# Raw weights in single blocks through four half-size buffers, a changed account of landings and readiness, and state-gate weights read again instead of kept

## The chip, the core and the metric

The kernel runs on one core of one Trainium2 chip. The metric is device time in microseconds (us) of one execution. The engines are named as the profile names them: PE (TensorE; PEld its weight loads), DVE (VectorE), ACT (ScalarE), POOL (GpSimd) and SP (SyncE, which here issues DMAs only).

## The reference

One layer of a hybrid encoder: 16 learned meta tokens stand ahead of 2048 frames of 1024 channels. The input is normalized and goes through one projection with seven parts of 512 columns; the result feeds a convolution group and a stick-breaking attention group, whose outputs are joined, projected, normalized and added to the input.

```python
u = rms_norm(h, pre_g)
proj = u @ w_in                      # 1024 x 3584
glu_a, glu_b, conv_gate, q, k, v, sb_gate = jnp.split(proj, ...)
c = glu_a * jax.nn.sigmoid(glu_b)
c = causal_depthwise_conv(c, conv_w, conv_b)          # width 31
c = jax.nn.silu(layer_norm(c, conv_ln_g, conv_ln_b))
c = (c @ w_pw2 + b_pw2) * jax.nn.silu(conv_gate)
s = stick_breaking_attention(heads(q), heads(k), heads(v))   # 8 heads of 64
s = s * jax.nn.silu(sb_gate)
mixed = jnp.concatenate([c, s], axis=-1) @ w_out      # 1024 x 1024
return h + rms_norm(mixed, post_g)

# within the attention
z = q @ k.T * scale
log_stay = where(visible, log_sigmoid(-z), 0)
tail = cumsum(log_stay, reverse=True) - log_stay
a = where(visible, exp(log_sigmoid(z) + tail), 0)
out = a @ v
```

All arrays are float32. The kernel gets near that accuracy by splitting each operand into a high part (rounded to the matmul's format) and a low part (the rest): high x high, high x low and low x high are three matmuls into one PSUM bank.

## The kernel before

**Tiling.** The frames are worked on in four chunks of 512 (`TC`), 128 rows at a time. For chunk c, `attention(c)` is the main stream of PE work: per head and block of keys it computes scores (`T<-kk,q`), turns the running products that DVE scans back (`T<-ident,pr`) and sums values (`av<-ah,vk`, `av<-al,vk`). Beside it a second stream, the fill, does the state gate `sb_gate(c)`, the output projection of chunk c - 1, the convolution's norm (`conv_norm`, with the transposes `T<-ident,acc`) and gate of chunk c, and the input projection of chunk c + 1 (`mm<-uh,w`, `mm<-ul,w`). The first input projection stands alone at the start (0 to about 140 us). By the trace the state gates are stored at 152 to 173, 372 to 400, 674 to 706 and 1018 to 1060 us, at the start of each chunk's fill.

**Who sets the order.** The program is written out by hand at build time. `Clock` and `Engine` hold an account with a cost for every instruction: when a tile is ready, when a buffer is free, how far each engine has come. `merge` and `either` take from the streams the one whose next piece is due (`need` gives that time), so PE's order is fixed by the account. Small work on other engines is a `Later`: what it reads, what it writes, a date before which it isn't issued, and the tag of a buffer that it needs. On the chip each engine runs its instructions in that fixed order and waits for what isn't there, and all that stand behind wait with it.

**Weights.** A weight block is 128 x 512 numbers. A raw block comes by `sp.dma_start` from `wpack` into a `wr` buffer. `split` makes the two parts: ACT copies the high part (`w<-wr`), POOL, or DVE for seven blocks at the start, subtracts it (`w<-wr,w`). They lie side by side in a `w` slot. Blocks that are needed in later chunks are written by POOL's queue to `wscr` in DRAM after the first split in chunk 0's fill or later, and the next uses load both parts at once (`w<-wscr`, 512 KB). There are four `w` slots (`WB`) and two `wr` buffers of two blocks (`RAWS`); when no raw block is left, the `wr` buffers serve as two more slots. In the trace the first such load is at 445 us. `weights` takes the next blocks for a product; `release` gives a slot back and calls `prepare` for the next block.

**Other names that the change touches.** `measure_later` loads 128 rows of x into a `q` buffer (`q<-x`) and has ACT sum their squares (`ev<-q`). `load_first_in` starts the kernel; there `times` multiplies the first x by the rate of each frame, the product standing in `pr` tiles. `turn` transposes the differences of the values (`T<-ident,ev`), which POOL has made from ACT's copy of the value projection (`ev<-mm`). `meta_v` brings the meta tokens' values into `vm`, sixteen loads in a row. `load_q` and `load_k` bring a head's queries and keys.

Of the kernel before, what the change touches and what calls it, by code (L numbers as in the profile page):

```python
# [11 lines left out]
F32 = mybir.dt.float32  # L12
F32R = mybir.dt.float32r
# [25 lines left out]

EV, WB, RAWS, PR, EHL = 5, 4, 2, 9, 4  # L40

# [126 lines left out]
class Engine:  # L168
# [7 lines left out]
    def __getattr__(self, name):  # L176
        call = getattr(self.engine, name)

        def issue(out, *args, **kw):
# [28 lines left out]
            return call(out, *args, **kw)  # L208
# [48 lines left out]
def trunk(ctx: ExitStack, tc: tile.TileContext, x, xturn, xlater, meta, cpack, post_g, wpack, out):  # L257
# [54 lines left out]
    def PT(tag, shape):  # L312
# [4 lines left out]
        return t  # L317

    def need(*aps, tag=None, given=None, evs=0, n=1):

        def at():
            if given and not given():
                return 1e6
            t = max([clock.at(a) for a in aps] + [0.0])
            if tag:
                t = max(t, clock.next_free(tag, n))
            if evs:

                t = max(t, clock.next_free("ev", evs) - 1.0)
            return t + 0.1

        return at
# [198 lines left out]
    at = {key: i for i, key in enumerate(slab_keys())}  # L533
    todo_raw = deque(zip(whole[::2], whole[1::2]))
    raws, ready, held, tags = deque(), deque(), [], deque()

    def load_raw(most=RAWS):

        while todo_raw and len(raws) < most:
            a, b = todo_raw.popleft()  # L540
            assert at[b] == at[a] + 1
            raw = T("wr", [P, 2, 4 * P], RAWS)
            sp.dma_start(raw, wpack[at[a] : at[a] + 2].rearrange("i p n -> p i n"))
            raws.append([raw, 0])

    def prepare(most=WB):

        while most and todo_w:
            if tags.count("w") < WB:
                tag, bufs = "w", WB  # L550
# [7 lines left out]
            both = T(tag, [P, 2, 4 * P], bufs, F32R)[:, :, :n]  # L558
            if kept:
                sp.dma_start(both.bitcast(F32), place[key][:, :, :n])  # L560
            else:
                if not raws:
                    load_raw()
                raw, i = raws[0]

                def keep_it(key=key, both=both):
                    when(
                        lambda: pool.dma_start(place[key], both.bitcast(F32)), [both[:, 1]]
                    )

                split(
                    raw[:, i], both[:, 0], both[:, 1],

                    dve if len(todo_w) in FIRST else pool,
                    keep_it if save else None,
                )
                raws[0][1] += 1
                if i:
                    raws.popleft()
                    when(  # L580
                        lambda: load_raw(min(RAWS, len(raws) + 1)), [],
                        date=0.0 if len(todo_w) in FIRST else pe.now + 2.0, tag="wr",
                    )
            ready.append(
                (key, [both[:, i].rearrange("p (k n) -> p k n", n=key[2]) for i in range(2)])
            )

# [54 lines left out]
    def load_first_in():  # L642
# [3 lines left out]
        uh, ul = u_now  # L646
        raw = T("wr", [P, 2, 4 * P], RAWS)
        raws.append([raw, 0])
        a, b = todo_raw.popleft()
        sp.dma_start(raw[:, 0], wpack[at[a]])  # L650
        sp.dma_start(cp, cpack)
# [4 lines left out]
        for k in range(KD):  # L656
            ts.append(T("pr", [P, TC], PR))
            sp.dma_start(ts[k], xturn[:, k, NM:])
            when(lambda k=k: part_in(0, k, ts[k], uh, ul), [ts[k], cp])
            if k == 0:  # L660
                sp.dma_start(raw[:, 1], wpack[at[b]])

# [49 lines left out]
        def spread():  # L712
# [101 lines left out]
    def measure_later(n):  # L814
# [18 lines left out]

        when(square, [t], [later[:, n : n + 1]], tag="ev")

# [53 lines left out]
    def qk_proj(c, g, scr, with_meta):  # L889
        for j in range(NJ):  # L890
# [99 lines left out]
    def values(c):  # L990
# [3 lines left out]
        for j in range(NJ):  # L994
# [27 lines left out]
            def turn(dv, j, rows, t0, nb):  # L1022
# [3 lines left out]
                for b in range(0, nb, 2):  # L1026
                    n = min(2, nb - b)
                    part = T("mixs", [P, 2, 4, HD], 8, F32R)[:rows, 0:n]
                    hi, lo = part[:, :, 0::3, :], part[:, :, 1:3, :]
                    d = pt[:, b : b + n].rearrange("p b (h d) -> p b h d", d=HD)  # L1030
                    act.activation(hi, d, AF.Copy)
# [25 lines left out]

    def meta_v():
        for j in range(NJ):
            force(f"v{j}")  # L1060
        for h in range(NH):
            e, j = h % 2, h // 2
            rows = slice(e * HD, (e + 1) * HD)
            for i in range(2):
                blk = (0 if i == 0 else 1) if e == 0 else (3 if i == 0 else 2)
                sp.dma_start(
                    vm[h * NM : (h + 1) * NM, i, j, rows].bitcast(F32),
                    vscr[j, 0:NM, blk * HD : (blk + 1) * HD],
                )

# [189 lines left out]
    def attention(c, mixs):  # L1260
# [156 lines left out]
        for i in range(len(order) + 1):  # L1417
            u = None
            if i < len(order):
                h, kc = order[i]  # L1420
                u = dict(h=h, kc=kc, diag=kc == c, kk=kk, a=[], at=[])
                if i + 1 < len(order):
                    if order[i + 1][0] != h:
                        heads[h + 1] = load_q(c, h + 1)
                    kk = load_k(*order[i + 1])
            for b in range(NTB if u else len(flips)):
                if u:
# [18 lines left out]
            if i == 1:  # L1446
# [10 lines left out]
                if c == 0:  # L1457
                    in_us(15.0, meta_v, outs=[vm])
            done = u
# [434 lines left out]
    with tc.manual_schedule(  # L1894
# [15 lines left out]
        for c in range(NCH):  # L1910
# [62 lines left out]
```

## Time and profile before

| what | value |
|---|---|
| median of 3 timed runs | 1337.16 us (1335.01, 1337.16, 1344.52) |
| profiled execution | 1343.13 us, its span 1341.4 us |
| PE busy | 1303.3 us, 97%, 7498 instructions |
| DVE, ACT, POOL busy | 76%, 54%, 48% |
| granted PE clock, mean | 0.99 |
| DMA | 311.23 MB, mean 232 GB/s |

The span runs from the first instruction to the last; the profiled execution's own time is 1.7 us longer. An engine's busy time is the time in which it executes; matmuls follow each other in a pipeline, so a single one is shown longer than its share. A wait stands as "who <- for whom: total us, times, longest us"; in the order of time each row has its start, its length, the engine, the instruction with its tiles, and in brackets the idle time before it and what ended it.

### The profile page before, as it was taken

What the parts mean: (1) busy time and instruction counts of PE and PEld (TensorE: products, weight loads), DVE (VectorE), ACT (ScalarE), POOL (GpSimd) and SP (SyncE); (2) the same over time, 40 slices, a digit from 0 to 9 for tenths busy, and PEclk for the clock granted to TensorE, in tenths of its full rate; (3) what the DMA queues carried; (4) which work ended last, traced back from release to release, by engine and by line L of the source; (5) the groups of instructions that cost most, each with busy time, mean ns of one, the idle gap of its engine ahead of it and who ended that gap; (6) DMA issues with size and microseconds to landing.
All of it is one profiled execution on the core that took longest, in us unless ns stands there. A gap on an engine that the chain in (4) does not pass through costs nothing.

```text
span 1341.4 us, 21636 instructions
## 1 busy us (share of the span) xinstructions
PE 1303.3 (97%) x7498; PEld 1117.9 (83%) x7498; DVE 1018.9 (76%) x1438; ACT 724.8 (54%) x1446; POOL 639.5 (48%) x764
## 2 busy tenths in 40 slices
PE   8998989999999999999999999999999999999897
PEld 8997877887789987888879987888777899988796
DVE  5997878998994378985495478885549989798865
ACT  6543436444445543576644454578676656655542
POOL 3554557767466631487721241399785121141300
PEclk9999989999999999999999999999999999999999
DMA  7575976999987896687866696667577455586655
GB/s 242 205 255 186 325 249 224 309 319 312 338 266 234 280 367 188 192 244 210 271 207 197 189 331 214 173 184 236 193 214 260 148 155 169 186 281 202 191 157 178
DMA packets 165501, 311.23 MB, mean 232 GB/s; under 512 B 16896, under 2 KB 71360, under 8 KB 165392
## 3 DMA queue, kind: packets, MB, share of 16 engines
q1 hardware_dynamic: 151088, 259.78, 62.0%
q0 software_dynamic: 14304, 50.08, 9.5%
q8 instruction: 59, 0.97, 0.3%
q14 instruction: 50, 0.41, 0.1%
HBM read 228.14 MB, written 81.66 MB: 231 GB/s over the span
## 4 chain that ended last, share of the span: by engine, by line
PE 76%; DVE 10%; DMA 6%; ACT 3%; issue 3%; POOL 2%; SPq 1%; DVEq 0%; ACTq 0%; POOLq 0%
PE mm L208 47%; PE T L208 20%; PE av L208 9%; DVE tok L208 2%; DVE ul L208 2%; DMA wr<-wpack 2%; DVE pr L208 2%; DVE cv L208 1%; DMA q<-x 1%; POOL w L208 1%; DVE al L208 1%; DMA w<-wscr 1%; ACT ev L208 1%; DMA ev<-post_g 1%; ACT uh L208 1%
## 5 line engine op out<-in xcount | busy, mean ns | idle before, releaser
L208 PE MATMUL mm<-uh,w 128*128 128x512 f32 (+1 forms) x1632 | 512.5, 374 | 3.1 <-ACT uh L208 2.1
L208 PEld LDWEIGHTS mm<-uh,w 128*128 128x128 f32 x1632 | 297.5, 191 | 51.5 <-ACT uh L208 2.3
L208 DVE TENSOR_TENSOR al<-T,ah 128x512 fp32r<-128x512 f32 (+3 forms) x323 | 194.1, 601 | 155.0 <-ACT ah L208 154.1
L208 PE MATMUL mm<-ul,w 128*128 128x512 f32 (+1 forms) x816 | 302.3, 370 | 3.4 <-DVE ul L208 3.4
L208 DVE TENSOR_TENSOR_SCAN pr<-T,pr,zcol 128x512 f32<-128x512 f32 x192 | 245.1, 1277 | 44.6 <-ACT T L208 42.4
L208 ACT ACTIVATE ah<-T 128x512 fp32r<-128x512 f32 (+3 forms) x323 | 172.0, 532 | 166.7 <-PE T L208 165.3
L208 DVE SCALAR_TENSOR_TENSOR cv<-ct,cp,cv 128x512 f32<-128x512 f32 x319 | 239.1, 750 | 7.1
L208 ACT ACTIVATE T<-T 128x512 f32<-128x512 f32 (+2 forms) x320 | 167.4, 524 | 92.0 <-PE T L208 88.1
L208 POOL TENSOR_TENSOR acc<-acc,pd 128x512 f32<-128x512 f32 x150 | 194.8, 1299 | 42.3 <-ACT pd L208 35.0
L208 PE MATMUL T<-kk,q 128*128 128x512 f32 (+2 forms) x640 | 196.4, 389 | 3.9 <-DVE al L208 3.2
L208 POOL TENSOR_TENSOR w<-wr,w 128x512 fp32r<-128x512 f32 x109 | 141.8, 1304 | 95.0 <-ACT w L208 92.8
L208 PEld LDWEIGHTS mm<-ul,w 128*128 128x128 f32 x816 | 155.9, 191 | 25.4 <-DVE ul L208 4.6
L208 PE MATMUL T<-ident,pr 128*128 128x128 f32 x1088 | 171.8, 273 | 1.6 <-DVE al L208 1.4
L208 PEld LDWEIGHTS T<-ident,pr 128*128 128x128 f32 x1088 | 134.2, 140 | 32.9 <-DVE al L208 3.1
L208 PEld LDWEIGHTS T<-kk,q 128*128 128x128 f32 x640 | 105.5, 190 | 18.2 <-DVE al L208 3.4
L208 DVE TENSOR_TENSOR_SCAN pr<-T,tri 128x128 f32<-128x128 f32 (+3 forms) x128 | 104.0, 814 | 20.6 <-ACT T L208 20.2
L208 PE MATMUL av<-ah,vk 128*128 128x512 f32 (+1 forms) x320 | 117.7, 368 | 1.0 <-ACT ev L208 1.0
L208 PE MATMUL av<-al,vk 128*128 128x512 f32 (+1 forms) x320 | 117.5, 367 | 0.0
L208 PE MATMUL mm<-uh,wr 128*128 128x512 f32 x320 | 115.8, 403 | 0.4 <-DVE mixc L208 0.4
L208 ACT ACTIVATE pd<-ct,cp 128x512 f32<-128x512 f32 x150 | 106.0, 718 | 18.0 <-POOL acc L208 16.9
L208 ACT ACTIVATE w<-wr 128x512 fp32r<-128x512 f32 x116 | 72.4, 627 | 74.3 <-DMA wr<-wpack 32.3
L208 POOL COPY cm<-pr 128x1 f32<-128x1 f32 x120 | 25.2, 213 | 135.5 <-DVE pr L208 132.0
(192 smaller groups left out, 1786.9 us busy)
## 6 DMA issues: line engine op xcount, KB each, us to landing
w<-wscr SPq DMA_DIRECT2D x128, 512.0 KB, 4.3
wscr<-w POOLq DMA_DIRECT2D x76, 512.0 KB, 5.5
wr<-wscr SPq DMA_DIRECT2D x62, 512.0 KB, 4.1
wr<-wpack SPq DMA_DIRECT2D x57, 512.0 KB, 5.0
kk<-kscr SPq DMA_DIRECT2D x80, 256.0 KB, 5.1
vk<-vscr SPq DMA_DIRECT2D x80, 256.0 KB, 4.1
q<-qscr SPq DMA_DIRECT2D x64, 256.0 KB, 6.1
vscr<-mixs SPq DMA_DIRECT2D x32, 256.0 KB, 4.0
```

The lines of the kernel that those rows point to most:

```text
L208: return call(out, *args, **kw)
```

## The change

- **Raw blocks singly.** `wr` becomes four buffers of one block, loaded one at a time; each comes free with its own split. When no raw block is left, two of them make one weight slot.
- **State-gate weights aren't kept.** The 32 blocks of the group `G_SG` take no part in `wscr`: they are read raw and split again in every chunk. So the last raw block is used in the state gate of chunk 3, and the fifth and sixth slot are there only from then on. Instructions: 24 more splits, 8 fewer writes to `wscr`, 140 loads of 128x512 in place of 57 of 128x2x512 and 2 of 128x512, and 172 loads' worth of kept blocks in place of 196.
- **The account.** From 30 us on a DMA is taken to land 1.0 us later than before, a raw block 2.5 us later, and a raw buffer to come free 3.0 us later. `need` asks for tiles to be ready 1.0 us before PE takes a piece, in place of 0.1; in the last chunk it is 0.1 again.
- **Dates and pieces.** The square of later rows gets a date 8 us after its load is issued; `meta_scores` 3 us in place of 1; `meta_v` goes head by head, 8 us apart, one load each; from chunk 1 on the next head's queries are loaded at a head's first key block; the first multiplication by the rates reads `row` in SBUF in place of the PSUM bank, and counts DVE's progress.

```diff
-EV, WB, RAWS, PR, EHL = 5, 4, 2, 9, 4
+EV, WB, RAWS, PR, EHL = 5, 4, 4, 9, 4
...
                 done = c.dma + 0.7
+                if start > 30.0:
+                    done += 2.5 if out.name.startswith("wr") else 1.0
...
             for a in (*outs, *near):
-                c.used[a.name] = max(c.used.get(a.name, 0.0), done)
+                late = 3.0 if a.name.startswith("wr") and start > 30.0 else 0.0
+                c.used[a.name] = max(c.used.get(a.name, 0.0), done + late)
...
+    slack = [1.0]
...
-            return t + 0.1
+            return t + slack[0]
...
-    again = [key for key, n in left.items() if n > 1]
+    again = [key for key, n in left.items() if n > 1 and not (key[0] == w_in and key[1] >= G_SG * P)]
...
         while todo_raw and len(raws) < most:
-            a, b = todo_raw.popleft()
-            assert at[b] == at[a] + 1
-            raw = T("wr", [P, 2, 4 * P], RAWS)
-            sp.dma_start(raw, wpack[at[a] : at[a] + 2].rearrange("i p n -> p i n"))
-            raws.append([raw, 0])
+            raw = T("wr", [P, 4 * P], RAWS)
+            sp.dma_start(raw, wpack[at[todo_raw.popleft()]])
+            raws.append(raw)
...
-            elif not (raws or todo_raw) and tags.count("wr") < RAWS:
-                tag, bufs = "wr", RAWS
+            elif not (raws or todo_raw) and tags.count("wr") < RAWS // 2:
+                tag = "wr"
...
-                raws[0][1] += 1
-                if i:
-                    raws.popleft()
-                    when(
-                        lambda: load_raw(min(RAWS, len(raws) + 1)), [],
-                        date=0.0 if len(todo_w) in FIRST else pe.now + 2.0, tag="wr",
-                    )
...
+                split(raws.popleft(), hi, lo, dve if first else pool, keep_it if save else None)
+                when(
+                    lambda: load_raw(min(RAWS, len(raws) + 1)), [],
+                    date=0.0 if first else pe.now + 2.0, tag="wr",
+                )
...
-                    lambda k=k: times(k, pt), [ts[k], pt], [ts[k]], date=pe.now + 3.0 + 1.5 * k
+                    lambda k=k: times(k), [ts[k], row], [ts[k]], dve, pe.now + 3.0 + 1.5 * k
...
-        def times(k, rates):
-            dve.tensor_tensor(ts[k], ts[k], rates, op=ALU.mult)
+        def times(k):
+            dve.tensor_tensor(ts[k], ts[k], row[:, NM:], op=ALU.mult)
...
-        when(square, [t], [later[:, n : n + 1]], tag="ev")
+        when(square, [t], [later[:, n : n + 1]], date=pe.now + 8.0, tag="ev")
...
-                    date=pe.now + 1.0,
+                    date=pe.now + 3.0,
...
-    def meta_v():
-        for j in range(NJ):
-            force(f"v{j}")
-        for h in range(NH):
...
+    def meta_v(h):
+        e, j = h % 2, h // 2
+        force(f"v{j}")
+        sp.dma_start(
+            vm[h * NM : (h + 1) * NM, :, j, e * HD : (e + 1) * HD].bitcast(F32),
+            vscr[j, 0:NM, e * P : (e + 1) * P].rearrange("s (i d) -> s i d", d=HD),
+        )
...
-                    if order[i + 1][0] != h:
+                    if c == 0:
                         heads[h + 1] = load_q(c, h + 1)
                     kk = load_k(*order[i + 1])
+                    if 0 < kc == c and h + 1 < NH:
+                        heads[h + 1] = load_q(c, h + 1)
...
-                    in_us(15.0, meta_v, outs=[vm])
+                    for h in range(NH):
+                        in_us(15.0 + 8.0 * h, lambda h=h: meta_v(h), outs=[vm[h * NM : (h + 1) * NM]])
...
             if c + 1 == NCH:
                 main = either(main, meta_late())
+                slack[0] = 0.1
```

What this does to the order of the instructions is shown at three places.

**ACT, second value projection of chunk 0 and after** (`ev,sq<-q` is the square of later rows, `ev<-mm` the copy of the value projection in two halves, `mixs<-T` the high part of the transposed differences). Before:

```order
L208 ACTIVATE mixs<-T 16x2x64
L208 ACTIVATE ev<-mm 128x264
L208 ACTIVATE ev,sq_102<-q_1288 128x1024
L208 ACTIVATE w<-wr 128x512
L208 ACTIVATE ev<-mm 128x264
L208 ACTIVATE w<-wr 128x512
L208 ACTIVATE mixs<-T 128x2x2x64 x2
```

Of the change:

```order
L211 ACTIVATE mixs<-T 16x2x64
L211 ACTIVATE ev<-mm 128x264
L211 ACTIVATE w<-wr 128x512
L211 ACTIVATE ev<-mm 128x264
L211 ACTIVATE w<-wr 128x512
L211 ACTIVATE ev,sq_102<-q_1318 128x1024
L211 ACTIVATE mixs<-T 128x2x2x64 x2
```

The square has moved from between the two copies to behind both.

**SP, the first chunk's attention, where the meta values are loaded** (`vm<-vscr`; `wr<-wpack` are raw weights, `vk`, `q` and `kk` the loads of attention). Before:

```order
L208 DMA gscr<-ev 128x512
L208 DMA wr<-wpack 128x2x512 x2
L208 DMA vm<-vscr 16x64 x16
L208 DMA wr<-wpack 128x2x512
L208 DMA vk<-vscr 128x4x128
L208 DMA q_2306<-qscr 64x2x512 x2
```

Of the change:

```order
L211 DMA gscr<-ev 128x512
L211 DMA wr<-wpack 128x512 x4
L211 DMA vm<-vscr 16x2x64
L211 DMA wr<-wpack 128x512 x2
L211 DMA vm<-vscr 16x2x64
L211 DMA vk<-vscr 128x4x128
L211 DMA q_2347<-qscr 64x2x512 x2
L211 DMA kk<-kscr 128x512
L211 DMA wr<-wpack 128x512
L211 DMA vm<-vscr 16x2x64
```

The sixteen loads in one piece are eight, each with raw weights between.

**PE and DVE, the transposes of the convolution's sums in chunk 0** (`T<-ident,acc` on PE reads the four `acc` tiles; the last of them is written on DVE by `acc<-ct_95,cp,cv`). PE before:

```order
L208 MATMUL av<-ah,vk 128x384
L208 MATMUL av<-al,vk 128x384
L208 MATMUL mm<-uh,w 128x512
L208 MATMUL mm<-ul,w 128x512
L208 MATMUL mm<-uh,w 128x512 x2
L208 MATMUL mm<-ul,w 128x512
L208 MATMUL mm<-uh,w 128x512
L208 MATMUL T<-ident,pr 128x128 x4
L208 MATMUL mm<-uh,w 128x512
L208 MATMUL mm<-ul,w 128x512
L208 MATMUL mm<-uh,w 128x512 x2
L208 MATMUL mm<-ul,w 128x512
```

(one more `mm<-uh,w` follows, and then the twelve `T<-ident,acc`.) PE of the change:

```order
L211 MATMUL av<-ah,vk 128x384
L211 MATMUL av<-al,vk 128x384
L211 MATMUL T<-ident,acc 128x128 x12
L211 MATMUL mm<-uh,w 128x512
L211 MATMUL mm<-ul,w 128x512
```

DVE before:

```order
L208 SCALAR_TENSOR_TENSOR cv<-ct_95,cp,cv 128x512 x5
L208 TENSOR_TENSOR mixc<-mm,mixc 128x512
L208 TENSOR_TENSOR al<-T,ah 128x128
L208 SCALAR_TENSOR_TENSOR pr<-T,tri 128x256
L208 SCALAR_TENSOR_TENSOR cv<-ct_95,cp,cv 128x512 x2
L208 SCALAR_TENSOR_TENSOR acc<-ct_95,cp,cv 128x512
```

DVE of the change:

```order
L211 SCALAR_TENSOR_TENSOR cv<-ct_95,cp,cv 128x512 x4
L211 SCALAR_TENSOR_TENSOR acc<-ct_95,cp,cv 128x512
L211 TENSOR_TENSOR mixc<-mm,mixc 128x512
L211 TENSOR_TENSOR al<-T,ah 128x128
L211 SCALAR_TENSOR_TENSOR pr<-T,tri 128x256
```

PE comes to the transposes twelve matmuls of 512 columns and four narrow ones earlier, DVE to the last sum before three of its other instructions.

More of the change, by code (lines that the diff above doesn't have):

```diff
@@ L533, in trunk @@
     at = {key: i for i, key in enumerate(slab_keys())}
-    todo_raw = deque(zip(whole[::2], whole[1::2]))
+    todo_raw = deque(whole)
     raws, ready, held, tags = deque(), deque(), [], deque()
@@ L557, in prepare @@
             key, n, kept, save = todo_w.popleft()
-            both = T(tag, [P, 2, 4 * P], bufs, F32R)[:, :, :n]
-            if kept:
+            if tag == "w":
+                both = T(tag, [P, 2, 4 * P], WB, F32R)[:, :, :n]
+                hi, lo = both[:, 0], both[:, 1]
+            else:
+                hi, lo = (T(tag, [P, 4 * P], RAWS, F32R)[:, :n] for _ in range(2))
+            if kept and tag == "w":
                 sp.dma_start(both.bitcast(F32), place[key][:, :, :n])
+            elif kept:
+                for i, t in ((0, hi), (1, lo)):
+                    sp.dma_start(t.bitcast(F32), place[key][:, i, :n])
             else:
@@ L646, in load_first_in @@
         uh, ul = u_now
[L647 to L650, printed above, removed]
+        load_raw(1)
         sp.dma_start(cp, cpack)
@@ L660, in load_first_in @@
             if k == 0:
-                sp.dma_start(raw[:, 1], wpack[at[b]])
+                load_raw(2)
         def meta_in():
@@ L1029, in turn @@
                     hi, lo = part[:, :, 0::3, :], part[:, :, 1:3, :]
+                    if rows == NM:
+                        hi, lo = part[:, :, 0::2, :], part[:, :, 1::2, :]
                     d = pt[:, b : b + n].rearrange("p b (h d) -> p b h d", d=HD)
```

26 lines of the change are left out of this document (5 added, 21 removed).

## The prediction

> **What bounds the kernel now.** I read the page first, then the table of stretches, then what TensorE (PE) waits for, then the order of time around its longest waits.
>
> ```profile
> span 1341.4 us, 21636 instructions
> PE 1303.3 (97%) x7498; PEld 1117.9 (83%) x7498; DVE 1018.9 (76%) x1438; ACT 724.8 (54%) x1446; POOL 639.5 (48%) x764
> ```
>
> PE is busy for 97% of the span, and the change leaves its matmuls as they are. Only its idle time (1341.4 - 1303.3 = 38 us) and the matmuls at a lowered clock can be won. The stretches say where that is (us; busy time and count of PE, PEld, DVE, ACT, POOL; granted clock; DMA share; GB/s).
>
> ```profile
> 0.00:100.00 100.00, 92.89 (x728) 91.06 (x729) 80.66 (x124) 56.13 (x108) 47.10 (x63) 0.98 0.69 235
> 100.00:150.00 50.00, 45.52 (x234) 37.72 (x233) 41.66 (x63) 20.58 (x44) 24.36 (x31) 0.97 0.71 234
> 150.00:200.00 50.00, 45.27 (x214) 36.96 (x213) 36.61 (x59) 15.58 (x33) 26.63 (x42) 0.93 0.78 274
> 200.00:250.00 50.00, 47.05 (x215) 38.06 (x214) 42.05 (x59) 29.18 (x56) 41.68 (x47) 0.97 0.74 248
> 250.00:1012.00 762.00, 756.70 (x4096) 635.83 (x4094) 547.62 (x766) 426.51 (x833) 426.27 (x484) 1.00 0.76 246
> 1012.00:1332.00 320.00, 315.90 (x2020) 278.31 (x2019) 265.29 (x361) 175.47 (x368) 71.91 (x98) 0.99 0.62 191
> 1332.00:1341.40 9.40, 0.02 (x1) 0.00 (x0) 4.98 (x12) 1.32 (x6) 1.54 (x2) 0.70 0.45 168
> ```
>
> PE idles 7.1 us in the first 100, 12.2 us from 100 to 250 (4.48 + 4.73 + 2.95), 5.3 us in the long stretch up to 1012, 4.1 us up to 1332, and 9.4 us in the tail after the last matmul. Between the start and the tail the clock falls most where PE idled most. So 150 us of the first chunk hold most of what can be won. By cause (total us, times, longest us):
>
> ```profile
> PE T L208 <- DVE al L208: 6.9, 5, 3.2
> PE T L208 <- POOL ev L208: 6.0, 5, 4.2
> PE mm L208 <- DVE ul L208: 3.4, 3, 2.3
> PE T L208 <- DVE ul L208: 1.7, 2, 1.0
> ```
>
> Each of the first three holds one long wait; I call them A (3.2 us), B (4.2) and C (2.3).
>
> **The change, part by part.** *Wait B: the squares of later rows.*
>
> ```profile
> 99.96 0.60 SPq L208 DMA_DIRECT2D q<-x  x1
> 106.02 1.06 ACT L208 ACTIVATE ev<-q 128x1024 bf16<-128x1024 f32 x1 [3.91 <-DMA q<-x]
> 107.59 0.37 ACT L208 ACTIVATE ev<-mm 128x264 f32<-128x264 f32 x1
> 108.98 1.07 POOL L208 TENSOR_TENSOR ev<-ev 128x528 f32<-128x528 f32 x1
> 110.11 1.06 PE L208 MATMUL T<-ident,ev 128*128 128x128 f32 x5 [4.19 <-POOL ev L208]
> ```
>
> The load of x left SP at 99.96 and its data came at 106.02, 6.1 us later. The square stood in ACT's queue ahead of the copy of a value projection (107.59), on which POOL's difference and PE's transposes wait. The date `pe.now + 8.0` puts the square behind that copy, and 8 us is more than this load took. The chain behind the copy then starts 3.91 + 1.06 = 5.0 us earlier (its matmuls stand ahead of PE's own wait), and PE's wait is 4.19: it goes, with a margin of 0.8. With it goes the first of these slow stretches:
>
> ```profile
> 110.00:114.00 4.00, 3.89 (x20) 3.82 (x21) 2.10 (x5) 2.31 (x6) 1.45 (x4) 0.57 0.34 82
> 185.00:192.00 7.00, 5.48 (x16) 4.60 (x17) 5.03 (x11) 2.24 (x5) 4.20 (x9) 0.54 0.24 87
> 216.00:220.00 4.00, 4.00 (x12) 3.14 (x12) 3.81 (x5) 1.75 (x3) 3.34 (x5) 0.57 0.28 113
> ```
>
> A clock of 0.57 over 4 us loses 0.43 x 4 = 1.7 us of work; after A it is 0.46 x 7 = 3.2 us, after C 1.7 again. For B I take 4.2 + 1.7 less 0.4 for the thin margin: **-5.5**; bounds -5.9 and 0.
>
> *Wait A: meta_v in one piece, raw weights in pairs.*
>
> ```profile
> 173.33 5.43 SPq L208 DMA_DIRECT2D wr<-wpack  x2
> 178.81 9.89 SPq L208 DMA_DIRECT2D vm<-vscr  x11
> 182.12 1.20 PE L208 MATMUL T<-ident,acc 128*128 128x128 f32 x9 [1.53 <-DVE acc L208]
> 184.62 0.63 ACT L208 ACTIVATE w<-wr 128x512 fp32r<-128x512 f32 x1 [8.10 <-DMA wr<-wpack]
> 185.77 0.69 DVE L208 TENSOR_TENSOR al<-T,ah 128x512 fp32r<-128x512 f32 x1 [3.70 <-ACT ah L208]
> ...
> 186.52 1.01 PE L208 MATMUL T<-kk,q 128*128 128x384 f32 x2 [3.19 <-DVE al L208]
> ```
>
> A pair's buffer comes free only when both its blocks are split; the second load of the first row left late, and the small loads of vm ran beside it. ACT stood 8.1 us at its first block; ah, al and PE's bank followed late. Now a buffer is free after each split, so a load has three blocks' time to come in and not two, and vm goes in eight loads 8 us apart. What the loads take (KB, median us to landing), and ACT's whole wait for them:
>
> ```profile
> wr<-wpack SPq DMA_DIRECT2D x57, 512.0 KB, 5.0
> wr<-wpack SPq DMA_DIRECT2D x2, 256.0 KB, 3.4
> w<-wscr SPq DMA_DIRECT2D x128, 512.0 KB, 4.3
> L208 ACT ACTIVATE w<-wr 128x512 fp32r<-128x512 f32 x116 | 72.4, 627 | 74.3 <-DMA wr<-wpack 32.3
> ```
>
> Two blocks are some 5 us here (the pair of loads lies within 5.43 us), so three are some 8, against 3.4 to 5.0 for a load. I take the wait and its slow clock as gone: 3.2 + 3.2 = **-6.4**; bounds -6.4 and 0. The 1.5 us at acc stay. PE now comes to its acc transposes twelve matmuls of 512 columns sooner (3.1 us, if twelve of half their width take 1.57, rows below), DVE to its acc three instructions sooner (by the row of al 0.69 + 0.69 + 0.2 for a narrow one, 1.6): 1.5 us more to wait. But DVE idles 8.3 us from 100 to 150 and PE 4.5, so with B gone DVE gets back more. I take **+1.0**; bounds 0 and +3.2, if a wait of 3.0 us lowers the clock too, as C's 2.3 us did. [...]
>
> *Wait C* is left at **0**; bounds -4 and +2:
>
> ```profile
> 212.89 2.91 DVE L208 SCALAR_TENSOR_TENSOR ul<-tok,cp,uh 128x512 fp32r<-128x512 f32 x2
> ```
>
> PE waits for the second of these. DVE computes the parts of u in the same place among its other work as before, and a margin in the account doesn't make them shorter.
>
> *Rates from SBUF.* Eight multiplications read `row` in place of a bank in PSUM. The nearest rows (ns: least, median, most; then the group with its mean):
>
> ```profile
> L208 DVE TENSOR_TENSOR tok<-tok,row x24: 675/682/1786, 62.6 to 813.1; 128x512 f32<-128x512 f32 x24
> L208 DVE TENSOR_TENSOR tok<-tok,row 128x512 f32<-128x512 f32 x24 | 18.2, 803 | 0.8 <-DMA tok<-xlater 0.7
> ```
>
> The least, 675, is what an undisturbed one takes, the mean is 803: 8 x 0.128 = **+1.0** us, all on the path, because PE already waits for ul behind them (1.7 us in the table of waits); bounds 0 and 8 x (1786 - 675) = +8.9. [...]
>
> *State-gate weights and slots.* Twenty-four more blocks are split, at 0.627 us on ACT and 1.304 on POOL (15 and 31 us), and eight wscr writes fall away. ACT and POOL are half idle, and these blocks stand in SBUF well ahead: 0, bounds 0 and +2. The price is elsewhere: spare wr buffers serve as fifth and sixth weight slots once no raw block is left, which was so from about 450 us and now is only past 1012. With four slots a load has the time of three blocks:
>
> ```profile
> 539.82 0.32 SPq L208 DMA_DIRECT2D w<-wscr  x1
> 543.30 0.32 SPq L208 DMA_DIRECT2D w<-wscr  x1
> ...
> 708.07 1.65 PE L208 MATMUL mm<-w,mixs 128*128 128x256 f32 x12
> 716.87 1.57 PE L208 MATMUL mm<-w,mixs 128*128 128x256 f32 x12
> ...
> SPq L208 <- PE av L208: 156.7, 54, 8.0
> L208 POOL TENSOR_TENSOR w<-wr,w 128x512 fp32r<-128x512 f32 x109 | 141.8, 1304 | 95.0 <-ACT w L208 92.8 <-PE T L208 1.5
> ```
>
> In the projections a block follows every 3.5 us, so three are 10.5; in the output projection the fifth block starts 716.87 - 709.72 = 7.2 us after the end of the first. A load takes 4.3, so both hold, but SP's queue can stand for up to 8.0 us behind a vk. I take **+1.5**; bounds 0 and +6.
>
> *The margin of 1 us* holds until chunk 3 and can only shorten waits of about a microsecond. Of the 5.3 us between 250 and 1012 I take **-2**; bounds -4 and +1. In chunk 3 it is 0.1 as before: 0, bounds -3 and +3 from another start. The loads of q that go earlier meet no wait of PE in the table: 0.
>
> Sum: -5.5 - 6.4 + 1.0 + 1.0 + 1.5 - 2 = **-10.4 us**. The profiled execution took 1343.13 us (1.7 around its span) and would take 1332.7. It is the second slowest of four; the median of the timed runs is 1337.16, and on that I predict 1326.8.
>
> **The rivals.**
> - *DVE sets the pace.* A and B go, but DVE, busy for 120 of the 150 us from 100 to 250, isn't early enough, and PE gives back half of the 11.9 us at acc and ul. For it: those waits stand there now. Against: DVE itself idled 3.70 us in A because of ACT. -10.4 + 6 gives 1332.8.
> - *The margin clears more.* C goes too (2.3 + 1.7), with 1.5 at acc and 1.5 more of the small waits: -17.4, 1319.8. Against it: DVE's work ahead of C is the same.
> - *Thin slots, slower.* Once per quarter of chunk 2's output projection a weight load stands 8.0 us behind a vk and lands after 12.3 us where 7.2 are there: 5 us, four times, each with 1.7 us of slow clock, 27 us. It decides once landing after release passes 7.2. -10.4 + 27 gives 1353.8. For it: SP's waits. Against: the landing of 4.3.
> [...]
> - *It doesn't do what it says.* x lands later than 8 us, or raw blocks still come late: A and B stay, about 1337.
>
> **How the numbers follow.** Chances: forecast 0.40 (1322 to 1331), DVE 0.18 (1329 to 1336), more 0.18 (1315 to 1323), slots 0.10 (1343 to 1365), port 0.06, no effect 0.08 (1333 to 1341). One per cent, about what a measurement of this kernel can tell from no change, is 13.4 us: 1323.8 and 1350.5. Faster by more: 0.17 of "more" and 0.10 of the forecast, 0.27. Slower by more: 0.07 of "slots". The rest, 0.66, lies within. The range 1316 to 1340 leaves out "slots" and the lower edge of "more", 0.13 together, and takes in the other bounds one at a time.
>
> **What the profile after would show.** Right: no wait of PE over 1.5 us for POOL ev near 105 or for al near 185; ACT's wait for raw weights down from 32.3 to under 12; PE idle from 100 to 250 down from 12.2 to about 5, with one slow stretch left, near C; waits of PE for weights between 450 and 1012 under 1 us; 133 instructions in POOL's w group. Wrong: PE waiting for w<-wscr in chunk 2's output projection (slots), pr<-pr,row at a mean over 1.2 us with a longer wait for ul near 50 (port), or the idle time of 100 to 250 back as waits for acc and ul (DVE).

## The result, and the profile after

| what | before | after |
|---|---|---|
| median, same chips | 1344.2 us (13 runs) | 1334.27 us (13 runs) |
| ratio, 95% interval | | 0.993 (0.9908 to 0.9953) |
| profiled execution, span | 1343.13, 1341.4 us | 1335.07, 1333.2 us |
| last matmul ends at | 1332.0 us | 1318.8 us |

About 9.4 us faster by the ratio. The level needs a word: the three runs at first gave 1337.16 for the kernel before, and ten more lifted its median to 1344.2; in the later comparisons it was 1342 to 1343. So ratios are compared below, not times. A trace is one execution; those of the changed kernel spread over 6 us and those of the kernel before over 16, so a difference of a few us between two traces counts only with the ratio or with the instructions that make it.

The page's first lines and the table of stretches of the changed kernel (columns as before):

```profile
span 1333.2 us, 21888 instructions
PE 1299.6 (97%) x7498; PEld 1115.9 (84%) x7498; DVE 1025.9 (77%) x1438; ACT 735.0 (55%) x1470; POOL 667.3 (50%) x780
```

```profile
0.00:100.00 100.00, 90.82 (x683) 87.58 (x684) 81.47 (x118) 52.89 (x100) 45.20 (x59) 1.00 0.68 224
100.00:150.00 50.00, 50.00 (x284) 42.64 (x283) 46.40 (x71) 23.74 (x52) 24.59 (x28) 1.00 0.72 223
150.00:200.00 50.00, 49.66 (x251) 41.07 (x249) 42.74 (x67) 24.58 (x49) 31.81 (x46) 1.00 0.83 265
200.00:250.00 50.00, 45.97 (x198) 36.47 (x199) 40.32 (x56) 22.79 (x45) 37.39 (x44) 0.93 0.66 229
250.00:1012.00 762.00, 758.06 (x4112) 638.26 (x4111) 554.23 (x773) 435.38 (x856) 452.92 (x505) 1.00 0.75 241
1012.00:1318.80 306.80, 305.08 (x1977) 269.83 (x1976) 255.76 (x348) 174.31 (x367) 73.86 (x98) 1.00 0.61 188
1318.80:1333.20 14.40, 0.04 (x1) 0.00 (x0) 5.00 (x12) 1.31 (x6) 1.53 (x2) 0.59 0.29 109
```

Length less the first number is PE's idle time: 9.2 us (7.1 before), 0, 0.3 (4.5 and 4.7 before), 4.0 (2.95), 3.9 (5.3), 1.7 (4.1). The idle time before the last matmul falls by 9.5 us, PE's busy time by 3.7 (1303.3 to 1299.6; up to the last matmul the clock was halved for 20.5 us before and for 6.8 after): the last matmul ends 13.2 us earlier. But the tail behind it has grown from 9.4 to 14.4 us. 13.2 less 5.0 is the 8.2 us by which the span is shorter. That tail is the surprise of this case.

What PE waits for, and the places of B, A and C:

```profile
PE mm L211 <- DVE ul L211: 5.3, 6, 2.4
PE mm L211 <- DVE ehl L211: 2.8, 4, 1.6
PE T L211 <- DVE ul L211: 2.6, 4, 0.8
...
PE mm L211 <- DMA w<-wscr: 1.4, 1, 1.4
PE T L211 <- POOL ev L211: 1.4, 3, 0.6
...
PE T L211 <- DVE al L211: 0.2, 1, 0.2
```

```profile
110.00:114.00 4.00, 4.00 (x36) 3.98 (x35) 3.80 (x6) 1.96 (x5) 2.32 (x4) 1.00 1.05 389
185.00:192.00 7.00, 7.00 (x36) 5.81 (x35) 6.84 (x11) 3.46 (x6) 2.82 (x5) 1.00 0.62 202
208.00:216.00 8.00, 6.81 (x17) 5.38 (x18) 4.12 (x7) 2.02 (x4) 4.59 (x7) 0.57 0.35 137
```

B (longest wait for ev 4.2, now 0.6) and A (al 3.2, now 0.2) are gone, with their slow clock. C stays, and its slow stretch is now 0.43 x 8 = 3.4 us of lost work, in place of 1.7. From 100 to 250 us PE idles 4.4 us (0.00 + 0.34 + 4.03), where about 5 were forecast. ACT's wait for raw weights fell from 32.3 to 5.0 us:

```profile
ACT w L211 <- DMA wr<-wpack: 5.0, 4, 1.7
```

The 133 splits on POOL that were foretold, in its group of the page:

```profile
L211 POOL TENSOR_TENSOR w<-wr,w 128x512 fp32r<-128x512 f32 x133 | 174.9, 1319 | 89.3 <-ACT w L211 88.1
```

### The profile page after: what moved, and what is told of

It reads as the page before. It is cut to its first block, busy times and chain, and to the rows that moved or that the text cites. A ratio compares the mean times of both kernels' runs of the same rounds, so it can differ in the third digit from the quotient of the medians.

```text
span 1333.2 us, 21888 instructions
## 1 busy us (share of the span) xinstructions
PE 1299.6 (97%) x7498; PEld 1115.9 (84%) x7498; DVE 1025.9 (77%) x1438; ACT 735.0 (55%) x1470; POOL 667.3 (50%) x780
## 3 DMA queue, kind: packets, MB, share of 16 engines
q0 software_dynamic: 13152, 45.88, 9.0%
## 4 chain that ended last, share of the span: by engine, by line
PE 84%; DVE 8%; DMA 3%; ACT 2%; issue 1%; POOL 1%; DVEq 0%; SPq 0%; POOLq 0%; ACTq 0%
PE mm L211 54%; PE T L211 20%; PE av L211 9%; DVE ul L211 2%; DVE tok L211 2%; DVE pr L211 1%; DVE cv L211 1%; DMA ev<-x 1%; DMA w<-wscr 1%; ACT ev L211 1%; DMA out<-tok 0%; DMA tok<-xlater 0%; PE cv L211 0%; DMA wr<-wscr 0%; DVE al L211 0%
## 5 line engine op out<-in xcount | busy, mean ns | idle before, releaser
L211 PE MATMUL mm<-uh,w 128*128 128x512 f32 (+1 forms) x1936 | 622.3, 378 | 4.5 <-DVE ehl L211 2.8
L211 PEld LDWEIGHTS mm<-uh,w 128*128 128x128 f32 x1936 | 354.7, 190 | 65.5 <-DVE ehl L211 2.8
L211 PE MATMUL mm<-ul,w 128*128 128x512 f32 (+1 forms) x968 | 362.7, 375 | 5.3 <-DVE ul L211 5.3
L211 POOL TENSOR_TENSOR w<-wr,w 128x512 fp32r<-128x512 f32 x133 | 174.9, 1319 | 89.3 <-ACT w L211 88.1
L211 PEld LDWEIGHTS mm<-ul,w 128*128 128x128 f32 x968 | 184.2, 190 | 34.5 <-DVE ul L211 8.6
L211 ACT ACTIVATE w<-wr 128x512 fp32r<-128x512 f32 x140 | 86.9, 626 | 48.2 <-PE mm L211 21.0
L211 POOL TENSOR_TENSOR ev<-ev 64x512 f32<-64x512 f32 (+2 forms) x46 | 55.9, 1216 | 68.1 <-ACT ev L211 52.2
```

## Experiments

Five rounds each beside the kernel before, unless said. First one part alone on the kernel before, then one part undone in the changed kernel.

**The square's date alone.**

```diff
-        when(square, [t], [later[:, n : n + 1]], tag="ev")
+        when(square, [t], [later[:, n : n + 1]], date=pe.now + 8.0, tag="ev")
```

> The kernel before with one edit: the square of later rows gets the date 8 us after its load. Theory (each part removes its own wait): PE's wait for POOL ev near 105 us (4.2 us) and the slow clock behind it (1.7) go, about 5 us faster than before; wait A for al near 185 (3.2 us and 3.2 of slow clock) stays. Rival (a new order as such, any edit shuffles the waits): wait B may stay, A may go, and the total is within 2 us of before. Rival (the account's margin does it all): no change.

Measured: ratio 0.998 (0.9953 to 1.0007). Waits of PE and ACT:

```profile
PE T L208 <- DVE al L208: 5.5, 5, 2.4
...
PE av L208 <- ACT ev L208: 3.8, 1, 3.8
PE T L208 <- POOL ev L208: 2.3, 5, 0.7
...
ACT w L208 <- DMA wr<-wpack: 33.9, 13, 6.3
```

The date removes B (0.7 us is left) and leaves ACT's wait for raw weights as it was. A doesn't quite stay as the theory had it: the wait for al there is 2.4 us in place of 3.2, and no half clock follows it. But the order behind it shifts, and a new wait of 3.8 us stands at 447 us; from 250 to 1012 us PE idles 10.1 us in place of 5.3, and most of the gain is lost again. The interval holds both the 5 us of the theory and no gain at all, so the time decides nothing here.

**The meta values head by head alone** (`meta_v(h)`, 8 us apart, and the parts that it reads, as in the change).

> The kernel before with one edit: the meta values come head by head, eight loads 8 us apart in place of sixteen in a row. Theory: the burst of vm loads on SP is gone, ACT's longest wait for raw weights falls from 8.1 to under 6 us, wait A shrinks or goes: 2 to 6 us faster; wait B stays. Rival (the pairs alone make A): ACT still waits over 6 us near 185 and the time is within 2 us of before.

Measured: ratio 1.0013 (0.9988 to 1.0039).

```profile
PE T L208 <- POOL ev L208: 5.7, 5, 3.8
...
ACT w L208 <- DMA wr<-wpack: 29.3, 13, 5.9
```

B stays, and ACT's wait hardly moves: by itself this part is worth nothing that can be measured. At A's place (188 us) 1.9 us of wait are left of 3.2, so the burst was some of A, not its core.

**Raw blocks singly, alone** (four buffers of one block; account, dates and kept blocks as before).

```diff
-EV, WB, RAWS, PR, EHL = 5, 4, 2, 9, 4
+EV, WB, RAWS, PR, EHL = 5, 4, 4, 9, 4
...
-            raw = T("wr", [P, 2, 4 * P], RAWS)
-            sp.dma_start(raw, wpack[at[a] : at[a] + 2].rearrange("i p n -> p i n"))
...
+            raw = T("wr", [P, 4 * P], RAWS)
+            sp.dma_start(raw, wpack[at[todo_raw.popleft()]])
...
```

> The kernel before with one edit: raw weights in single blocks through four half-size buffers; the account, the dates and the kept state-gate weights are as before. Theory: ACT's wait for raw weights falls from 32 to under 12 us, wait A (al near 185) goes: 4 to 7 us faster, wait B stays. Rival (the burst of vm makes A): ACT still waits over 5 us once near 185, within 2 us of before.

Measured: ratio 0.9976 (0.9951 to 1.0001).

```profile
PE mm L208 <- DVE ul L208: 4.0, 3, 3.6
...
PE T L208 <- POOL ev L208: 2.3, 5, 0.7
PE T L208 <- DVE al L208: 2.3, 3, 1.5
...
ACT w L208 <- DMA wr<-wpack: 2.9, 2, 1.8
```

ACT's wait for raw weights goes from 32.3 to 2.9 us, and both A and B are gone, though the square has no date here. The price is at C: 3.6 us for ul. The edit makes the loads half as large and frees each buffer by itself; which of the two ends ACT's wait was not separated.

**The account alone** (later landings, raw buffers free later, margin 1.0; pairs as before).

> The kernel before with the account alone changed: landings later by 1.0 (raw 2.5), raw buffers free 3.0 later, margin 1.0 until the last chunk. Theory: the margin shortens only small waits; B (4 us, ACT behind the load of x) stays, A may shrink: 0 to 4 us faster. Rival (the account does it all): A and B both under 1.5 us, 8 us faster or more.

Measured: ratio 1.0131 (1.0097 to 1.0165), 17 us slower.

```profile
PE T L211 <- DVE pr L211: 6.5, 10, 1.4
PE T L211 <- POOL ev L211: 5.5, 5, 1.9
PE mm L211 <- ACT w L211: 4.3, 4, 1.3
PE mm L211 <- POOL w L211: 4.0, 7, 0.9
```

Neither text fits: the longest waits for ev and al fall to 1.9 and 1.0 us, and yet the kernel is slower. PE waits 8.3 us for split weights, where the changed kernel's table has no such row, while ACT waits for raw blocks for 5.6 us only. Our reading, which no run shows by itself, is that with pairs an account that frees buffers late puts the splits late in the order. Which of the account's numbers does it was not separated. Nor is this all of it: PE's idle time up to the last matmul grows by 8.5 us, its busy time by 9.7, and 6.8 us more of half clock account for only 3.4 of that; the rest is open.

**The square's date taken back in the changed kernel** (the edit of the first run, reversed).

> The changed kernel with one part undone: the square of later rows has no date again. Two theories of wait B. (1) The date cures it, as the prediction had it: the wait of TensorE for POOL's ev near 105 to 110 us comes back with 3 to 4 us and a stretch of half clock behind it, the first 200 us cost 4 to 6 us more, and the ratio to the kernel before goes from 0.993 to about 0.997. (2) The raw blocks in singles cure it by themselves, as the run with single blocks alone suggests (no wait for ev over 0.7 us there): no wait over 1.5 us for ev near 105, and the time within 1.5 us of the changed kernel, ratio 0.992 to 0.994.

Measured: ratio 0.9935 (0.9909 to 0.996), the changed kernel's own.

```profile
PE T L211 <- POOL ev L211: 3.8, 5, 1.2
```

Two waits of about 1.2 us come back, 2.4 us of idle time from 100 to 150, and PE still ends 1.2 us earlier than in the changed kernel. The second theory holds in the time: with single blocks the date is worth nothing more.

**The margin taken back.**

```diff
-    slack = [1.0]
+    slack = [0.1]
```

> The changed kernel with one part undone: the margin of readiness is 0.1 us throughout instead of 1.0 until chunk 3. Theory (the margin is worth about what the prediction gave it): waits of about a microsecond come back in chunks 0 to 2, idle time of TensorE from 250 to 1012 rises from 3.9 to 5 to 7 us, and the ratio goes from 0.993 to 0.9945 to 0.996. Rival (the margin does nothing here, or costs, as the run of the account alone on the kernel before, 1.3% slower, would allow): idle time from 250 to 1012 stays within 1 us of 3.9 or falls, ratio 0.991 to 0.994.

Measured: ratio 0.9989 (0.9969 to 1.001). From 250 to 450 us in the changed kernel, then in this one:

```profile
250.00:450.00 200.00, 200.00 (x1158) 172.18 (x1157) 157.59 (x233) 98.78 (x216) 138.46 (x174) 1.00 0.87 290
```

```profile
250.00:450.00 200.00, 195.04 (x1109) 166.87 (x1108) 151.79 (x225) 94.50 (x208) 131.83 (x168) 0.99 0.83 283
```

The theory holds, and its size was too small: 5.0 us of idle time come back there (and a half clock of 3.4 us at 340), the last matmul ends 6.3 us later, and the whole gain of the change is gone.

**The later landings taken back** (both additions to `done` and to `c.used`; the margin stays).

> The changed kernel with the later landings of the account undone (DMAs land in the account as before, raw buffers come free as before); the margin of readiness, the single raw blocks and all else stay. Theory (with single blocks the landing account matters little, since single blocks alone took ACT's wait for raw weights from 32.3 to 2.9 us): idle time of TensorE within 3 us of the changed kernel's, ratio 0.991 to 0.995. Rival (it is the landing account that keeps raw weights and x off the engines that wait for them): ACT's waits for DMA grow to over 15 us, a wait of TensorE of 2 us or more comes back between 100 and 200 us, ratio 0.996 or more.

Measured: ratio 0.9965 (0.9946 to 0.9983), the last matmul 3.5 us later.

```profile
PE mm L208 <- DVE ul L208: 6.1, 4, 4.2
```

The ratio is the rival's, its mechanism isn't. ACT's waits for DMA stay small (wr<-wpack 4.8 us), and no wait comes back between 100 and 200 us. Where the time goes shows only in part: C is longer (4.2 us in place of 2.4), and from 250 to 1012 us PE idles 6.1 us in place of 3.9, with 0.9 us for split weights at 426.

**VectorE dearer in the account** (`scalar_tensor_tensor` of 128x512 at 0.78 us in place of 0.665).

> The changed kernel, with the account's cost of a VectorE scalar_tensor_tensor of 128x512 raised from 0.665 to 0.78 us, which is what they take from start to start in the trace of the changed kernel. Theory (the waits that are left, for ul at 41 to 57 and 199 to 209 us and for ehl at 73 to 75, come from an account that takes VectorE for faster than it is): with true costs TensorE is given other work ahead of those pieces, the wait C (2.6 us, with 6.8 us of half clock behind it) falls under 1 us, waits for ul go from 7.9 us in all to under 5, and the ratio goes from 0.993 to about 0.990. Rival (VectorE is at its limit there and nothing else can be put ahead): the waits for ul stay within 1 us of 7.9 in all or move to other places, ratio 0.992 to 0.996.

Measured: ratio 0.9999 (0.9975 to 1.0023). C goes, as the theory said, and the stretch around it gets worse:

```profile
200.00:250.00 50.00, 39.31 (x210) 31.38 (x209) 46.14 (x78) 32.33 (x68) 31.77 (x53) 0.90 0.53 149
```

PE idles 10.7 us there, at al, bst, acc and ev, with DVE busy for 46 of 50 us: the rival's mechanism, for this stretch. The ratio lies above what both texts gave.

**State-gate weights kept again** (`again` as before).

> The changed kernel with one part undone: the state-gate weights are kept in DRAM again, so the wr buffers serve as a fifth slot from chunk 1 on. Theory (thin slots, small): the one wait for w<-wscr at 731.8 us (1.4 us in the table) goes, idle time of TensorE from 250 to 1012 falls from 3.9 to about 2.5 us, POOL's busy time falls by some 25 to 31 us from 667, and the ratio goes from 0.993 to 0.992. Rival (re-reading is worth something by itself, since it takes writes and 512 KB reads out of the queues): waits for weights or for kk appear between 250 and 700 us, and the ratio is 0.996 or more.

Measured: ratio 0.9905 (0.9878 to 0.9933). The wait for w<-wscr goes and POOL's busy time falls by 27 us, as the theory had it. But the last matmul comes at 1319.2, no earlier than in the changed kernel. What is gained is behind it: 8.2 us to the end in place of 14.4. That led to the next three.

**The tail.** SP's rows for the last four writes, before and after:

```profile
1335.16 2.32 SPq L208 DMA_DIRECT2D out<-ul  x4
```

```profile
1321.99 2.32 SPq L211 DMA_DIRECT2D out<-ul  x4
```

In both the last of them is issued 5.5 us after the last matmul. Before, the end comes 3.9 us after that, in the changed kernel 8.9. In between no engine executes any work. SP waits until the writes have landed (the last of them 3.2 us after its issue, at 1340.3 us, before; 2.1 us after it, at 1326.1, in the changed kernel), and POOL stands in its closing DRAIN, for which the views have no row. By the records of the instructions in the traces, SP was through at 1340.5 us in the kernel before and POOL's DRAIN at 1336.5; in the changed kernel SP was through at 1326.6 and the DRAIN only at 1332.4. So the landing of the last writes sets the end before, and the DRAIN sets it after:

```
kernel                       DMAs issued by POOL   closing DRAIN   last matmul to end
before                       130                    2.01 us         9.3 us
kept again                   130                    2.01            8.2
after                        122                   11.08           14.4
after, margin taken back     122                   11.08           14.4
24 writes moved to SP         98                    9.12           12.4
six small writes more        128                   11.57           14.9
eight small writes more      130                    1.85            8.7
```

In all of them POOL issues its last DMA 94 us or more before the DRAIN, and in the traces of before and after none of POOL's DMAs took more than 8.9 us to land, the last one 4.6 and 4.9, so it isn't a write of POOL's on its way that the DRAIN waits for. The first four rows gave the suspicion; the runs of the last three tested it. Eight writes of 16 rows that nothing reads:

```diff
+    marks = dr.tile([8, 16, 4 * P], F32, name="marks")
+    marked = deque(range(8))
...
+                def mark(lo=lo):
+                    i = marked.popleft()
+                    when(lambda: pool.dma_start(marks[i], lo[0:16].bitcast(F32)), [lo])
...
```

> The changed kernel with eight small writes more from POOL's queue: 16 rows of 2 KB of the first eight state-gate blocks into a place in DRAM that nothing reads. In every trace of a kernel that issues 130 DMAs from POOL's queue the closing DRAIN of POOL takes 2.01 us, in all four with 122 (the changed kernel and three variants) 11.08 us, and the kernel ends 14.4 us after the last matmul instead of 8.2 to 9.3. Theory (the number of DMAs on POOL's queue sets it): with 130 the drain is 2.0 us again, the time from the last matmul to the end 8.2 us, and the ratio to the kernel before 0.988 to 0.990 (6 us less than the changed kernel), with the 24 more splits on POOL still there. Rival 1 (the bytes or packets of POOL's queue set it, 50.08 MB and 14304 packets before, 45.88 and 13152 after): the drain stays near 11 us, ratio 0.993. Rival 2 (the 24 more splits on POOL set it): the same, 11 us and 0.993.

Measured: median 1326.46 us, ratio 0.9867 (0.9836 to 0.9898): the fastest kernel of the study, ahead of both.

```profile
1315.90:1324.60 8.70, 0.02 (x1) 0.00 (x0) 4.99 (x12) 1.31 (x6) 1.54 (x2) 0.76 0.48 181
```

The DRAIN took 1.85 us in place of 11.08. What decides here is the number of POOL's DMAs, 130 in place of 122, not the bytes (45.88 MB before the small writes, 46.15 with them) and not the 24 splits, which are still there. 5.7 of the 8 us to the changed kernel are this tail; PE also ends 2.9 us earlier, which the tail can't explain and which stays open.

The 24 writes of finished rows issued by SP, three rounds:

```diff
-                lambda: pool.dma_start(out[t0 : t0 + P, i * 512 : i * 512 + 512], o), [o]
+                lambda: sp.dma_start(out[t0 : t0 + P, i * 512 : i * 512 + 512], o), [o]
```

> The changed kernel with the 24 writes of finished rows (out<-tok) issued by SP instead of POOL, so POOL's queue issues 98 DMAs instead of 122. For the length of POOL's closing DRAIN. Theory a (it grows with the number of DMAs since the last multiple of 128: 2 of 130 give 2.01 us, 122 give 11.08, so 0.0755 us each over 1.86): 98 give 9.3 us, and the kernel ends 12.6 us after the last matmul. Theory b (a threshold: below some number between 122 and 130 the drain takes 11 us whatever the number): 11.1 us and 14.4 us. Theory c (the kind of the last or of the output writes sets it, not the number): 2 us and about 8.3 us. The total time is of less interest, since SP's queue takes 24 more writes: ratio 0.990 to 1.0.

Measured: DRAIN 9.12 us, ratio 0.9903 (0.9867 to 0.9938). Theory a, within 0.2 us; of its 128 this run shows nothing.

Six small writes and a margin of 1.6 us:

> The changed kernel with two edits that are read apart: six small writes more from POOL's queue, 128 DMAs in all, and a margin of readiness of 1.6 us instead of 1.0 in chunks 0 to 2. The drain: theory (it counts DMAs since the last multiple of 128; 130 with eight small ones gave 1.85 us, 122 gave 11.08, 98 gave 9.12) 1.1 to 1.9 us, and 8.0 to 8.7 us from the last matmul to the end; rival (the step lies at 129 or 130) 11.5 us, and 14.8 us to the end. The margin: theory (it takes waits of up to its own size, and those that are left from 250 to 1012 us are mostly the short gaps between matmuls, so there is little more to win) TensorE idle from 250 to 1012 us within 1.5 us of 3.2 (the run with eight small writes), last matmul within 3 us of 1315.9, and the ratio to the kernel before 0.985 to 0.990; rival (each tenth of margin is worth what the first nine were, some 0.7 us) last matmul near 1312, ratio 0.983 or less.

Measured: DRAIN 11.57 us, 14.9 us to the end; last matmul at 1319.7, PE idle 5.5 us from 250 to 1012; ratio 0.9947 (0.993 to 0.9965). For the drain the rival is right: the step lies at 129 or 130, not at 128. The slope is 24 DMAs of 256 KB for 1.96 us and six of 32 KB for 0.49: 0.082 us for each at both sizes. For the margin neither text fits quite: nothing more was won, and PE idled 2.4 us longer from 250 to 1012 than with eight small writes and a margin of 1.0.

## Why the prediction was right or wrong

The forecast was a gain of 10.4 us by the profiled execution; measured are 8.1 there, and 9.4 by the ratio. The two main terms, A and B, were right, but the total is as close as it is by luck: up to the last matmul the gain was 13.2 us, more than the sum had, and the tail, for which the sum had nothing, took 5.0 of it back. The level of 1326.8 was 7.5 us low, nearly all of it the base: the three runs of before that it stood on were 7 us under the median of thirteen.

- **Wait B, -5.5:** right: 4.5 us of idle time from 100 to 150 and a slow stretch. The reason was half of it. The date suffices (first run), but so do the single blocks without it (third run).
- **Wait A, -6.4:** right. The third run shows that the pairs make it; that it is their buffer which comes free late, and not the size of their loads, was argued only. The +1.0 for acc was wrong: PE waits for acc nowhere now.
- **Wait C, 0:** wrong: it grew by 1.1 us of idle time and 1.7 us of slow clock, past its bound of +2. So was the reason, "DVE's work ahead of C is the same". What C is can be seen in the order of time of DVE, POOL and PE there, in the changed kernel and in the one with kept blocks:

```profile
204.57 4.57 DVE L211 SCALAR_TENSOR_TENSOR ul<-tok,cp,uh 128x512 fp32r<-128x512 f32 x2
...
205.50 0.56 POOL L211 DMA_DIRECT2D wscr<-w  x1 [0.30 <-POOL w L211]
...
206.08 1.29 POOL L211 TENSOR_TENSOR mixs<-acc,mixs 128x512 fp32r<-128x512 f32 x1
...
207.32 1.26 POOL L211 TENSOR_TENSOR w<-wr,w 128x512 fp32r<-128x512 f32 x1
...
209.19 0.80 PE L211 MATMUL mm<-ul,w 128*128 128x512 f32 x1 [2.43 <-DVE ul L211]
```

```profile
203.00 0.57 POOL L211 DMA_DIRECT2D wscr<-w  x1 [0.30 <-POOL w L211]
...
203.18 5.93 DVE L211 SCALAR_TENSOR_TENSOR ul<-tok,cp,uh 128x512 fp32r<-128x512 f32 x2
...
203.60 1.28 POOL L211 TENSOR_TENSOR w<-wr,w 128x512 fp32r<-128x512 f32 x1
...
204.83 1.26 POOL L211 TENSOR_TENSOR mixs<-acc,mixs 128x512 fp32r<-128x512 f32 x1
...
206.03 0.56 POOL L211 DMA_DIRECT2D wscr<-w  x1
...
206.62 1.27 POOL L211 TENSOR_TENSOR mixs<-acc,mixs 128x512 fp32r<-128x512 f32 x1
...
208.50 0.79 PE L211 MATMUL mm<-ul,w 128*128 128x512 f32 x1 [5.33 <-DVE ul L211]
```

  One undisturbed `ul` takes 0.74 us. Taken singly in the trace, the second of the two in the first fence takes 3.47, the first of the two in the second 5.27, and each ends some 0.55 us after POOL's last instruction in a row without a gap. In the kernel before it was 2.25, beside a DMA issue and one more POOL instruction. In twelve of the fourteen traces one `ul` there takes 2.2 us or more, and each of the twelve ends 0.56 us after POOL's last instruction; PE's longest wait goes with it, 2.3 us for a `ul` of 2.25, 2.4 for 2.86 and 3.47, 3.6 for 4.67, 4.2 to 5.3 for 5.27. So C follows POOL's run of instructions beside it, which is how its size could change from kernel to kernel. This is read from overlaps; no run moved POOL's work alone.
- **Rates from SBUF, +1.0:** mis-sized for the same reason. After, and before (least, median, most in ns):

```profile
L211 DVE TENSOR_TENSOR pr<-pr,row x9: 282/1134/1582, 30.2 to 44.0; 128x512 f32<-128x512 f32 x8, 128x128 f32<-128x128 f32 x1
```

```profile
L208 DVE TENSOR_TENSOR pr<-pr,cv x8: 674/678/679, 29.0 to 34.1; 128x512 f32<-128x512 f32 x8
```

  The eight take 8.9 us (mean 1110 ns) in place of 8 x 0.678 = 5.4, and the reads from PSUM stood at 0.68 us beside such POOL splits: +3.5 on DVE. Three of the eight took 0.68: one that met no POOL instruction, one that met one only in its last 0.06 us, and one beside a POOL instruction that began 0.08 us after it; the other five, each beside one or two POOL instructions, took 1.13 to 1.58. PE's idle time in the first 100 us grew by 2.1. The median of 682 misled: 13 of the 24 instructions behind it met no POOL instruction, seven of the other eleven took under 0.70 us beside one, and four took 0.97 to 1.79.
- **Slots, +1.5:** right in size: one wait of 1.4 us at 732 us, in chunk 2's output projection. The text had waits for weights under 1 us as a sign of being right and a wait at this place as a sign of "Thin slots", so that sign spoke for the rival. With kept blocks the wait goes; with eight small writes it is gone too, with the slots as few, so four slots alone don't make it.

```profile
728.16 0.32 SPq L211 DMA_DIRECT2D w<-wscr  x1
...
733.60 1.68 PE L211 MATMUL mm<-w,mixc 128*128 128x256 f32 x12 [1.44 <-DMA w<-wscr]
```

- **The eight wscr writes that fall away, 0 with a bound of +2:** the step that failed. They cost 5.0 us, at an end of the kernel for which the sum had no term: POOL's DRAIN took 11.08 us in place of 2.01.
- **The margin, -2:** too small. Idle time from 250 to 1012 fell by only 1.4 against the kernel before (5.3 to 3.9), but without the margin it is 9.5, and the last matmul comes 6.3 us later. The later landings were not priced apart; they are worth 3.5 us to the last matmul.
- **The last chunk, 0 with bounds of -3 and +3:** missed. PE's idle time there fell by 2.4 us (4.1 to 1.7), and with it went a wait for al of 2.3 us at 1254 us and the 3.4 us of half clock behind it. Why that wait goes was not tested.
- **The rivals.** DVE doesn't set the pace as that rival had it: PE gives back nothing at acc from 100 to 250, and what it gives back at ul, at C, goes with POOL. "The margin clears more" needed C to go, and it stayed. "Thin slots" stayed at one wait in place of four. For "port" in the chances, no run shows a port; what the runs showed is that the eight multiplications took 3.5 of the bound of 8.9 us more on DVE, at a mean of 1.11 us, under the sign of 1.2. PE's longest wait for a DVE instruction beside POOL was at C, 2.4 us in the changed kernel, and C was left at 0.

## What to carry to other kernels

Price the end of a kernel as a stretch of its own: here it was 8.2 to 9.3 us long with 130 DMAs issued by POOL and 12.4 to 14.9 with 98 to 128, with no wait of PE to show it. When a wait on VectorE changes its size with every reordering, as C did from 2.3 to 5.3 us, look at how long the awaited instruction itself took and what POOL ran beside it, before taking its queue for the cause. And parts of a change to an account need each other: later landings and a margin together lost 17 us with pairs in a buffer, and in the changed kernel, with single blocks, each was a gain (3.5 and 6.3 us to the last matmul).

## What the runs showed of the hardware

- POOL's closing DRAIN took 9.12, 11.08 and 11.57 us with 98, 122 and 128 DMAs issued by POOL, 0.082 us for each, and 1.85 to 2.01 us with 130. What happens between 128 and 130 was not seen; numbers well above 130 were not tried.
- A VectorE instruction of 128x512 (`ul<-tok,cp,uh`, in the kernel with kept blocks) took 5.27 us in place of 0.74 beside five POOL instructions in a row, two DMA issues among them, and ended 0.56 us after the last of them.
- Waits of PE of 2.3 and 2.4 us were followed by half clock at some places and not at others: 2.4 us for ul at C, with shorter ones before it, by 6.8 us of it in the changed kernel. The same wait of 2.4 us was followed by 3.4 us with eight small writes and without the square's date, and by 6.8 with the 24 writes on SP. A wait of 2.3 us at 1254 us in the kernel before, with only 0.2 us more beside it, was followed by 3.4 us; one of 2.4 us at 178 us in the run with the square's date alone by none. So in these traces the length of a wait alone doesn't decide.
